# A 21st weight slot in the MoE ring, tiles that share buffers, and the last output in halves

## The chip, the cores and the metric

The kernel runs on one core of a Trainium2 chip. The metric is the device time of the whole program in microseconds (us). The kernel before takes 1551.59 us, the median of three runs (1550.2 to 1551.77). The engines are PE (matrix multiply; PEld is its weight load), DVE and ACT (elementwise work, ACT with lookup functions), POOL, and SP, which here only issues DMA transfers. An engine executes its own instructions strictly in order and waits on semaphores for the others.

## The reference

One sequence of 256 tokens with 1024 features goes through two transformer blocks, all in fp32.

```
first_block:   x += [pool_mixer(u), attention(q, k, v)] @ w_out     # u, q, k, v = rms_norm(x) @ w_in; q, k normed, rotated
               x += cross_attention(rms_norm(x), rms_norm(mem))     # 4 heads, 256 memory rows
               x += conv_ffn(rms_norm(x))                           # d_ff 2816, causal conv of width 3
second_block:  x += g1 * rms_norm([MLA attention with ctx, fourier_mix] @ w_out)
               x += g2 * rms_norm(moe(modulate(x)))
moe:           logits = h @ w_router + b_router; the top 4 of 32 experts, gates = softmax of the 4
               g = min(x_e @ w_gate[e] + b_gate[e], 7); u = clip(x_e @ w_up[e] + b_up[e], -7, 7)
               y_e = (g * sigmoid(1.702 g) * (u + 1)) @ w_down[e] + b_down[e]       # 1024 x 1024 matrices
               y[token] += gate * y_e
```

## The kernel before

**The first part** (0 to about 600 us) is everything up to the router. Its weights come in chunks of 1 MB through a ring of four slots. ACT and DVE split each chunk into a high part `wh` (L325) and a low part `wl` (L326), in two half chunks each, and PE multiplies with three matmuls per product (`ah*wh`, `al*wh`, `ah*wl`; L432 to L434 and L439 to L441). The work is written as a list of steps, and a scheduler turns the list into one fixed order per engine at build time. SP's loads use eight DMA semaphores in turn, so that a load also waits for the one eight loads before it. Among the first steps are the query and key norms of the attention: DVE reduces squares (L575), takes a reciprocal square root (L306 to L314), scales a PSUM bank `ps_a` into `qn` (L581), which frees the bank, and rotates it (L595 to L600). A little later come the softmax of the second pair of heads (L622 to L640, exponentials on ACT at L636), and the pool mixer: ACT copies `pooled` out of PSUM twice (L681), and PE multiplies each copy with `poolw` (L690).

**The MoE part** (from about 600 us to the end) is a loop over 32 experts. Each has 12 chunks of 1 MB: four of w_gate, four of w_up, four of w_down. They are streamed in that order through a ring of 20 slots (`slots`, L1482), whose memory becomes free piece by piece as the first part ends: `b1`, `b2` and `b3` are opened as pools close, `a` is the ring of the first part, `x` one more slot. `load_to` (L1491, DMA at L1504) issues the next load on SP after the last matmul that reads the slot's old chunk. For each expert `hidden` (L1602) does eight short bias matmuls (L1608) and 64 matmuls of 128x512 on gathered tokens (L1615), and DVE and ACT make the SwiGLU from two PSUM tiles (`hg`, `hs`, `hu`, L1621 to L1627); `turned` transposes the result (L1634) and copies it into `aT` (L1635); `project` does 32 matmuls (L1647); ACT copies into `z` (L1720). Every second expert, `add_y` (L1656) adds two experts' results into four PSUM banks that stay open for the whole part, and `part` gathers the next pair's tokens (L1558). `extra` (L1659) runs for an expert with more than 64 tokens; it does so once here (33 groups of 64 matmuls at L1615 in all).

**The end** (L1722 to L1737): for each half of the tokens, the last `add_y`, ACT's squares `ysq` (L1729), DVE's product with the gate (L1730), the reciprocal square root, one DVE operation of 128x1024 that scales and adds the residual (L1735), and one 512 KB store (L1737).

Small tensors that are kept all the time (`con`: identity, ones, two index rows, a triangle; `vec`, `qkb`, `wrt`) lie in the pool `keep`. The working tiles of the MoE part lie in the pool `mw`, where tiles of one tag share that tag's buffers.

Of the kernel before, what the change touches and what calls it, by code (L numbers as in the profile page):

```python
# [15 lines left out]
ALU = mybir.AluOpType  # L16
# [19 lines left out]
for _n, _w in (("mix_g", 8), ("xattn_g", 8), ("mem_g", 8), ("ffn_g", 8), ("pre_g", 8), ("pool_s", 4),  # L36
# [4 lines left out]
NVEC = _o  # L41


CONS = {"con": (("ident", 128), ("ones", 128), ("iota1", 64), ("iota32", 32), ("upper", 128)),
        "conA": (("band", 4 * 384), ("mask", 256), ("rope_c", 128), ("rope_s", 128)),
        "conM": (("dft", 2 * 512), ("cc", 128), ("sc", 128), ("ax_c", 64), ("ax_s", 64))}
CON = {}
# [207 lines left out]
def network(ctx: ExitStack, tc: tile.TileContext, A):  # L255
# [28 lines left out]
        return new(pools["stage"], shape, dt, **kw)  # L284

    con = {"con": new(keep, [P, NCON["con"]], name="con")}
    vec = new(keep, [P, NVEC], name="vec")

    def C(name, n, off=0, rows=slice(None)):
        t, o = CON[name]  # L290
# [39 lines left out]


    open_pool("tail", side="right")()
    open_pool("base", side="right")()
    open_pool("psum", space=bass.MemoryType.PSUM)()

# [5 lines left out]
    W = {}  # L341

    con["conA"] = new(keep, [P, NCON["conA"]], name="conA", tag="k8a")
    qkb = new(keep, [P, 128 + NE], name="qkb")
    qkg = qkb[:, :128].rearrange("p (a b) -> p a b", a=2)
    brt = qkb[:, 128:]
    wrt = new(keep, [P, KD, NE], name="wrt")
    bexp = new(keep, [P, 512], name="bexp")
    cT = new(pools["tail"], [P, 8, 32], name="cT", bufs=1)
    wf = new(pools["tail"], [P, 2, P], name="wf", bufs=1)  # L350
# [4 lines left out]
    def late_loads():  # L355
# [5 lines left out]
    load(xT[:, :4], A["xT"][:, :4])()  # L361
    beside = {0: [load(xT[:, 4:], A["xT"][:, 4:])],
              1: [load(con["con"], A["con"]),
                  load(qkb, bass.AP(tensor=A["qkb"].tensor, offset=A["qkb"].offset, ap=[[0, P], [1, 128 + NE]]))],
              3: [load(con["conA"], A["conA"])],
              4: [lambda: load(S["poolw"], A["pool_w"])(), load(cT, A["cT"])]}
# [1112 lines left out]
    seq = [(e, m, c) for e in experts for m in range(3) for c in range(4)]  # L1479
    chunk = {}  # L1480
    state = {"n": 0}
    slots = ["b1"] * RING_B[0] + ["a"] * 2 + ["b2"] * RING_B[1] + ["a"] * (RING_A - 2) + ["b3"] * RING_B[2] + ["x"]  # L1482
    rings = {"a": ring[0], "x": ringx}

    def moe_open(name):
        n = int(name[1])
        rings[name] = ctx.enter_context(tc.tile_pool(name="ring" + name, bufs=RING_B[n - 1], side="left",
                                                     reuse_waits="tile"))
        load_to((RING_B[0] + 2, RING_B[0] + 2 + RING_B[1], len(slots))[n - 1])

    def load_to(n):  # L1491
        while state["n"] < min(n, len(seq)):
# [17 lines left out]
    close_pool("tail")()  # L1510
    x4 = S["x4"]

    mw = ctx.enter_context(tc.tile_pool(name="mw", bufs=1, side="right", reuse_waits="tile"))
    pm = ctx.enter_context(tc.tile_pool(name="pm", bufs=1, space=bass.MemoryType.PSUM, reuse_waits="tile"))

# [19 lines left out]
    def select(es, b):  # L1535

        n = len(es)
        rank = rp1
        if b:
            rank = new(small, [P, 2, NE], name="rank")  # L1540
            nc.vector.tensor_scalar(rank, rp1, float(-SLOTS * b), None, op0=ALU.add)
        sel = new(mw, [P, 2, n, SLOTS], name="sel%d" % n)
        for t in range(2):
            for i, e in enumerate(es):
                nc.vector.tensor_scalar(sel[:, t, i], C("iota1", SLOTS), rank[:, t, e:e + 1], scale4[:, t:t + 1],
                                        op0=ALU.is_equal, op1=ALU.mult)
        per = 512 // (n * SLOTS)
        xs = []

        def part(q):  # L1550

            if not xs:
                xs.append(new(mw, [P, KD, n * SLOTS], name="xs%d" % n))
            ps = pbank("t", 2)
            for i in range(per):
                j = q * per + i
                for t in range(2):
                    nc.tensor.matmul(ps[:, i * n * SLOTS:(i + 1) * n * SLOTS], x4[:, t, j * P:(j + 1) * P],  # L1558
                                     sel[:, t].rearrange("p a b -> p (a b)"), start=t == 0, stop=t == 1)
            for i in range(per):  # L1560
                j = q * per + i
                src = ps[:, i * n * SLOTS:(i + 1) * n * SLOTS]
                if j % 2:
                    nc.vector.tensor_scalar(xs[0][:, j], src, A2[:, j:j + 1], sh2[:, j:j + 1], op0=ALU.mult, op1=ALU.add)
                else:
                    nc.scalar.activation(xs[0][:, j], src, AF.Identity, bias=sh2[:, j:j + 1], scale=A2[:, j:j + 1])  # L1566
            return xs[0]
        return rank, part
# [7 lines left out]
    def spread(rank, es, orders=2):  # L1576

        n = len(es)
        gps = []
        for o in range(orders):  # L1580
            gp = new(mw, [P, 2, 2, SLOTS], name="gp", bufs=2)
            for t in range(2):
                for h in range(2):
                    e = es[(h + o) % n]
                    nc.vector.tensor_scalar(gp[:, t, h], C("iota1", SLOTS), rank[:, t, e:e + 1], G[:, t, e:e + 1],
                                            op0=ALU.is_equal, op1=ALU.mult)
            gps.append(gp)

        def turn():
            ps = pbank("t", 2)  # L1590
            for o, gp in enumerate(gps):
                for t in range(2):
                    nc.tensor.transpose(ps[:, o * T + t * P:o * T + (t + 1) * P], gp[:, t].rearrange("p a b -> p (a b)"), ident)

            def kept(tag):
                gt = new(mw, [P, orders, T], name="gt", tag=tag, bufs=3 if tag == "h" else 1)
                nc.vector.tensor_copy(gt, ps[:, :orders * T].rearrange("p (o n) -> p o n", o=orders))
                return gt
            return kept
        return turn  # L1600

    def hidden(e, xs, i, used=None):  # L1602

        res = [pbank("g", 2) for _ in range(2)]
        for m, ps in enumerate(res):
            for h in range(2):
                k, r = slice(64 * m, 64 * m + 64), 64 * m + 2 * e + h
                nc.tensor.matmul(ps[64 * h:64 * h + 64, :], ident[k, r:r + 1].to_broadcast([64, SLOTS]), bexp[k, :],  # L1608
                                 start=True, stop=False)
        for m, ps in enumerate(res):  # L1610
            for c in range(4):
                w = chunk[e, m, c]
                for jj in range(2):
                    for h in range(2):
                        last = nc.tensor.matmul(ps[64 * h:64 * h + 64, :], xs[:, 2 * c + jj, i * SLOTS:(i + 1) * SLOTS],  # L1615
                                                w[:, jj, 512 * h:512 * h + 512], start=False, stop=c == 3 and jj == 1)
                if used is not None:
                    load_to(used + 4 * m + c + 1 + len(slots))
            if m == 0:
                g = new(mw, [P, 512], name="hg", tag="h", bufs=3)  # L1620
                nc.vector.tensor_scalar(g, ps, 7.0, None, op0=ALU.min)  # L1621
                s = new(mw, [P, 512], name="hs", tag="h", bufs=3)
                nc.scalar.activation(s, g, AF.Sigmoid, scale=1.702)  # L1623
                nc.vector.tensor_tensor(g, g, s, op=ALU.mult)
        u = new(mw, [P, 512], name="hu", tag="h", bufs=3)
        nc.vector.tensor_scalar(u, res[1], 7.0, -7.0, op0=ALU.min, op1=ALU.max)  # L1626
        nc.vector.scalar_tensor_tensor(g, u, 1.0, g, op0=ALU.add, op1=ALU.mult)  # L1627
        return g, last.ins
# [30 lines left out]
    def extra(e, b, inner=None):  # L1659

        rank, xs = select_all([e], b)
        a, last = hidden(e, xs, 0)
        if inner:
            with tc.issue_after(last):
                tc.mark_branch_hint_location(inner, "LikelyTaken", [PE])
        z = new(mw, [P, 512], name="zx", tag="h", bufs=3)
        nc.scalar.activation(z, project(e, turned(a)), AF.Copy)
        gt = spread(rank, [e], 1)()("h")
        for t in range(2):
            for h in range(2):  # L1670
                r = slice(64 * h, 64 * h + 64)
                nc.tensor.matmul(yb[t][h], gt[r, 0, t * P:(t + 1) * P], z[r, :], start=False, stop=False,
                                 skip_group_check=True)
# [50 lines left out]
    for t in range(2):  # L1724
        s = new(small, [P, 2], name="cs_s")
        add_y(gt, z, t, True)
        for h, ps in enumerate(yb[t]):
            c = slice(512 * h, 512 * h + 512)
            nc.scalar.activation(new(mw, [P, 512], name="ysq", tag="h", bufs=3), ps, AF.Square, accum_out=s[:, h:h + 1])  # L1729
            nc.vector.tensor_tensor(y[:, t, c], ps, S["gate", 1][:, c], op=ALU.mult)  # L1730
        s2 = new(small, [P, 1], name="lat_s")
        nc.vector.tensor_tensor(s2, s[:, 0:1], s[:, 1:2], op=ALU.add)  # L1732
        r2 = rms_scale(s2, D, 1, "y")
        y3 = y[:, t].rearrange("p (q j) -> p q j", j=KD)
        nc.vector.scalar_tensor_tensor(y3, y3, r2, x4[:, t].rearrange("p (j q) -> p q j", j=KD),  # L1735
                                       op0=ALU.mult, op1=ALU.add)
        nc.sync.dma_start(out[t * P:(t + 1) * P, :], y[:, t])  # L1737


def arrays_of(i):  # L1740
# [48 lines left out]
```

## Time and profile before

| what | value |
|---|---|
| median of three runs | 1551.59 us |
| the profiled execution's own time, and its span | 1554.47 us, 1552.5 us |
| mean granted PE clock over the span | 0.983 |
| PE busy | 1465.9 us, 94% |
| DVE, ACT busy | 603.9 us, 39%; 431.3 us, 28% |
| DMA | 514.82 MB, mean 332 GB/s |

All durations below come from the profiled execution, which took 1554.47 us: 1552.5 us of span and 1.97 us around it. In the profile's 40 slices PE is at 8 or 9 tenths from the first to the last, the DMA engines are at 9 tenths only from the 17th slice on (the MoE weights, about 425 GB/s), and DVE and ACT, at 5 to 8 tenths in the first third, drop to 1 or 2 in the MoE part. A wait row names who released the waiting engine; only waits on the engine that the others follow cost time.

### The profile page before, as it was taken

The page shows a single profiled execution, that of the slowest core. Times are in us where ns is not written, and L with a number is a line of the kernel's source. Part 1 is how long each engine was busy: PE and PEld are TensorE (multiplying, and loading weights), DVE is VectorE, ACT ScalarE, POOL GpSimd, SP SyncE. Part 2 cuts the span into 40 slices and gives each one's busy share as a digit, 9 for nine tenths or more (in the row PEclk, how much of TensorE's full clock was granted, in tenths as well). Part 3 has the DMA queues.
Part 4 walks back from the last instruction along what each step waited for, and adds up shares of the span by engine and source line. Part 5 has one row for each costly group of instructions (what it writes and reads, how often), then busy time and mean ns, then how long its engine had stood idle before and what let it go on. Part 6 is the DMA issues. An engine that isn't in the chain of part 4 may idle for free. (4 is left out here: it accounts for less than half of the span.)

```text
span 1552.5 us, 20127 instructions
## 1 busy us (share of the span) xinstructions
PE 1465.9 (94%) x7985; PEld 831.0 (54%) x7985; DVE 603.9 (39%) x1436; ACT 431.3 (28%) x781; POOL 5.1 (0%) x13
## 2 busy tenths in 40 slices
PE   7999999999999998999999999999899999999996
PEld 5787888789998765333433333333334333333332
DVE  7859668666767465122212112112121122121113
ACT  5545655544547542111101111101111011011111
POOL 0000000000000000000000000000000000000000
PEclk9989999999999998999999999999999999999999
DMA  9645465886532448999999999999999999999993
GB/s 345 234 159 173 153 222 194 316 300 230 190 123 94 163 170 334 388 425 425 426 424 427 424 426 426 424 425 426 408 415 425 425 426 424 426 425 426 424 426 148
DMA packets 72883, 514.82 MB, mean 332 GB/s; under 512 B 8112, under 2 KB 8880, under 8 KB 11920
## 3 DMA queue, kind: packets, MB, share of 16 engines
q1 hardware_dynamic: 71712, 507.80, 80.8%
q0 software_dynamic: 1008, 4.78, 0.8%
q8 instruction: 110, 1.80, 0.4%
q14 instruction: 53, 0.43, 0.1%
HBM read 511.50 MB, written 1.05 MB: 330 GB/s over the span
## 5 line engine op out<-in xcount | busy, mean ns | idle before, releaser
L1615 PE MATMUL p_g<-w,xs 128*64 128x512 f32 x2112 | 461.1, 594 | 0.7 <-issue 0.7
L1615 PEld LDWEIGHTS p_g<-w,xs 128*64 128x64 f32 x2112 | 148.7, 137 | 310.8 <-issue 295.8
L1647 PE MATMUL p_t<-w,aT 128*64 128x512 f32 x1056 | 235.4, 598 | 2.2 <-ACT aT L1635 2.2
L326 DVE TENSOR_TENSOR wl<-w,wh 128x1024 fp32r<-128x1024 f32 (+3 forms) x150 | 173.1, 1178 | 50.2 <-ACT wh L325 50.0
L325 ACT ACTIVATE wh<-w 128x1024 fp32r<-128x1024 f32 (+3 forms) x150 | 146.8, 1016 | 132.9 <-issue 39.0
L1621 DVE TENSOR_SCALAR hg<-p_g 128x512 f32<-128x512 f32 x33 | 22.8, 692 | 378.9 <-PE p_g L1615 378.9
L1647 PEld LDWEIGHTS p_t<-w,aT 128*64 128x64 f32 x1056 | 73.2, 137 | 149.3 <-issue 130.1
L439 PE MATMUL ps_a<-wh,ah 128*128 128x512 f32 (+3 forms) x240 | 92.1, 387 | 12.7 <-ACT wh L325 11.1
L432 PE MATMUL ps_m<-ah,wh 128*128 128x256 f32 x352 | 101.6, 289 | 1.4 <-ACT wh L325 1.4
L1623 ACT ACTIVATE hs<-hg 128x512 f32<-128x512 f32 x33 | 20.8, 629 | 289.9 <-DVE hg L1621 289.9
L434 PE MATMUL ps_m<-ah,wl 128*128 128x256 f32 x352 | 100.4, 285 | 0.0
L433 PE MATMUL ps_m<-al,wh 128*128 128x256 f32 x352 | 100.4, 285 | 0.0
L1720 ACT ACTIVATE z<-p_t 64x512 f32<-64x512 f32 x63 | 37.3, 592 | 207.5 <-PE p_t L1647 207.1
L441 PE MATMUL ps_a<-wl,ah 128*128 128x512 f32 (+3 forms) x240 | 92.3, 385 | 0.0
L440 PE MATMUL ps_a<-wh,al 128*128 128x512 f32 (+3 forms) x240 | 91.8, 383 | 0.0
L1626 DVE TENSOR_SCALAR hu<-p_g 128x512 f32<-128x512 f32 x33 | 22.8, 692 | 154.7 <-PE p_g L1615 154.7
L1656 PE MATMUL p_y<-z,gt 128*128 128x512 f32 x128 | 63.9, 605 | 18.8 <-ACTq L1680 18.1
L1558 PE MATMUL p_t<-sel,x 128*128 128x128 f32 (+1 forms) x544 | 70.7, 285 | 11.2 <-ACT aT L1635 11.2
L1558 PEld LDWEIGHTS p_t<-sel,x 128*128 128x128 f32 x544 | 64.7, 195 | 28.6 <-issue 14.6
L1566 ACT ACTIVATE xs<-p_t,modT,A 128x128 f32<-128x128 f32 (+1 forms) x68 | 30.8, 453 | 158.9 <-PE p_t L1558 146.7
L432 PEld LDWEIGHTS ps_m<-ah,wh 128*128 128x128 f32 x352 | 68.1, 194 | 9.3 <-issue 3.4
L434 PEld LDWEIGHTS ps_m<-ah,wl 128*128 128x128 f32 x352 | 68.1, 194 | 2.4 <-DVE wl L326 0.8
(368 smaller groups left out, 1787.1 us busy)
## 6 DMA issues: line engine op xcount, KB each, us to landing
w<-w_gate_dram SPq DMA_DIRECT2D x128, 1024.0 KB, 19.6
w<-w_up_dram SPq DMA_DIRECT2D x128, 1024.0 KB, 19.5
w<-w_down_dram SPq DMA_DIRECT2D x127, 1024.0 KB, 19.6
w<-wall_dram SPq DMA_DIRECT2D x89, 1024.0 KB, 4.9
w<-wall_dram SPq DMA_DIRECT2D x4, 768.0 KB, 4.1
w<-wall_dram SPq DMA_DIRECT2D x3, 576.0 KB, 3.8
w<-wall_dram SPq DMA_DIRECT2D x2, 640.0 KB, 3.9
xT<-xT_dram SPq DMA_DIRECT2D x2, 512.0 KB, 7.7
```

Of the source, the lines that this page charges most:

```text
L325: nc.scalar.activation(hi, src, AF.Copy)
L326: nc.vector.tensor_tensor(lo, src, hi.bitcast(F32), op=ALU.subtract)
L432: nc.tensor.matmul(o, sh, mh, start=start, stop=False, **kw)
L433: nc.tensor.matmul(o, sh, ml, start=False, stop=False, **kw)
L434: nc.tensor.matmul(o, sl, mh, start=False, stop=stop, **kw)
L439: nc.tensor.matmul(o, a, wh, start=start, stop=False)
L440: nc.tensor.matmul(o, b, wh, start=False, stop=False)
L441: return nc.tensor.matmul(o, a, wl, start=False, stop=stop)
L1558: nc.tensor.matmul(ps[:, i * n * SLOTS:(i + 1) * n * SLOTS], x4[:, t, j * P:(j + 1) * P], sel[:, t].rearrange("p a b -> p (a b)"), start=t ...
L1615: last = nc.tensor.matmul(ps[64 * h:64 * h + 64, :], xs[:, 2 * c + jj, i * SLOTS:(i + 1) * SLOTS], w[:, jj, 512 * h:512 * h + 512], start= ...
L1647: nc.tensor.matmul(po[64 * h:64 * h + 64, :], s, w[:, jj, o:o + 512], start=c == 0 and jj == 0, stop=c == 3 and jj == 1)
L1656: nc.tensor.matmul(yb[t][h], gt[:, h, t * P:(t + 1) * P], z[:, h], start=False, stop=stop, skip_group_check=True)
```

## The change

- `con` is cut in two: `con` keeps the identity and the 64-wide index row, a new tensor `conR` holds the ones, the 32-wide index row and the triangle. `conR` gets a load of its own at the start, right behind `con`'s.
- `conR`, `vec`, `qkb` and `wrt` move from `keep` to `tail`, a pool that is closed before the MoE part.
- In the MoE part tiles are put under shared tags: `sel1` with `gp`, `xs1` with `aT`, `hu` and `zx` with `hs`, the `gt` of an extra pass with `hg`, `ysq` with `xs2`. Before, `hg`, `hs`, `hu`, `zx` and `ysq` went round three buffers of the tag `h`.
- The memory won becomes a 21st ring slot, `c`, opened when `tail` is closed; its first load is issued then.
- The last operation on DVE is done in two halves of 128x512 for each half of the tokens, and each half is stored by itself (four stores of 256 KB, not two of 512 KB).

```diff
-CONS = {"con": (("ident", 128), ("ones", 128), ("iota1", 64), ("iota32", 32), ("upper", 128)),
+CONS = {"con": (("ident", 128), ("iota1", 64)),
+        "conR": (("ones", 128), ("iota32", 32), ("upper", 128)),
...
-    vec = new(keep, [P, NVEC], name="vec")
...
     open_pool("tail", side="right")()
+    vec = new(pools["tail"], [P, NVEC], name="vec", bufs=1)
+    con["conR"] = new(pools["tail"], [P, NCON["conR"]], name="conR", bufs=1)
...
-    qkb = new(keep, [P, 128 + NE], name="qkb")
+    qkb = new(pools["tail"], [P, 128 + NE], name="qkb", bufs=1)
...
-    wrt = new(keep, [P, KD, NE], name="wrt")
+    wrt = new(pools["tail"], [P, KD, NE], name="wrt", bufs=1)
...
               1: [load(con["con"], A["con"]),
+                  load(con["conR"], A["conR"]),
...
-    slots = [... + ["b3"] * RING_B[2] + ["x"]
+    slots = [... + ["b3"] * RING_B[2] + ["x", "c"]
...
-        load_to((RING_B[0] + 2, RING_B[0] + 2 + RING_B[1], len(slots))[n - 1])
+        load_to((RING_B[0] + 2, RING_B[0] + 2 + RING_B[1], len(slots) - 1)[n - 1])
...
     close_pool("tail")()
     x4 = S["x4"]
+    rings["c"] = ctx.enter_context(tc.tile_pool(name="ringC", bufs=1, side="left", reuse_waits="tile"))
+    load_to(len(slots))
...
-                g = new(mw, [P, 512], name="hg", tag="h", bufs=3)
+                g = new(mw, [P, 512], name="hg")
...
-                s = new(mw, [P, 512], name="hs", tag="h", bufs=3)
+                s = new(mw, [P, 512], name="hs")
...
-        u = new(mw, [P, 512], name="hu", tag="h", bufs=3)
+        u = new(mw, [P, 512], name="hu", tag="hs")
...
-            nc.scalar.activation(new(mw, [P, 512], name="ysq", tag="h", bufs=3), ps, AF.Square, accum_out=s[:, h:h + 1])
+            nc.scalar.activation(new(mw, [P, 512], name="ysq", tag="xs2"), ps, AF.Square, accum_out=s[:, h:h + 1])
...
-        nc.vector.scalar_tensor_tensor(y3, y3, r2, x4[:, t].rearrange("p (j q) -> p q j", j=KD),
-                                       op0=ALU.mult, op1=ALU.add)
-        nc.sync.dma_start(out[t * P:(t + 1) * P, :], y[:, t])
+        for h in range(2):
+            q = slice(64 * h, 64 * h + 64)
+            nc.vector.scalar_tensor_tensor(y3[:, q], y3[:, q], r2, x4[:, t].rearrange("p (j q) -> p q j", j=KD)[:, q],
+                                           op0=ALU.mult, op1=ALU.add)
+            nc.sync.dma_start(out[t * P:(t + 1) * P, 512 * h:512 * h + 512], y[:, t, 512 * h:512 * h + 512])
```

Line numbers grow by 2 or 3 in the first part and by 3 to 7 in the MoE part (L581 becomes L584, L681 becomes L684, L1504 becomes L1507, L1737 becomes L1744). The scheduler places the same steps differently in the first 95 us; from there to the end PE's instructions come in the same order in both kernels. Three places follow.

The first place is DVE at about 33 to 40 us, the query norm beside the split of a weight chunk; `wl` is the low part of half a chunk, `rs_y` the reciprocal square root, `hs` a sum of squares. Before:

```order
L326 TENSOR_TENSOR wl<-w,wh 128x1024 [waits DMAHW3_49,PE_49,Activation_49]
L314 SCALAR_TENSOR_TENSOR rs_y_269<-rs_t_271,rs_y_269 128x8 [waits DVE_49]
L313 TENSOR_TENSOR rs_t_301<-rs_t_301,rs_h_300 128x8 [waits DVE_49]
L326 TENSOR_TENSOR wl<-w,wh 128x1024 [waits Activation_49]
L580 TENSOR_SCALAR rs_y_269<-rs_y_269,R_x_195 128x8 [waits DVE_49]
L314 SCALAR_TENSOR_TENSOR rs_y_299<-rs_t_301,rs_y_299 128x8 [waits DVE_49]
L575 TENSOR_REDUCE hs_402<-hsq 128x8 [waits Activation_49]
L581 TENSOR_TENSOR qn<-ps_a,rs_y_269 128x512 [waits DVE_49]
L580 TENSOR_SCALAR rs_y_299<-rs_y_299,R_x_195 128x8 [waits DVE_49]
```

And now:

```order
L326 TENSOR_TENSOR wl<-w,wh 128x1024 [waits DMAHW4_49,PE_49,Activation_49]
L583 TENSOR_SCALAR rs_y_271<-rs_y_271,R_x_197 128x8 [waits DVE_49]
L583 TENSOR_SCALAR rs_y_301<-rs_y_301,R_x_197 128x8 [waits DVE_49]
L584 TENSOR_TENSOR qn<-ps_a,rs_y_271 128x512 [waits DVE_49]
L326 TENSOR_TENSOR wl<-w,wh 128x1024 [waits Activation_49]
L598 TENSOR_TENSOR rot<-qn,rope 128x512 [waits DVE_49]
L600 TENSOR_TENSOR rotb<-qn,rope 128x8x32 x2
L578 TENSOR_REDUCE hs_404<-hsq 128x8 [waits Activation_49]
L603 TENSOR_TENSOR rot<-rot,rotb 128x512 [waits DVE_49]
```

The scaling `qn`, which empties a PSUM bank, stood behind both `wl` and behind the reduction at L575; now it stands behind the first `wl` alone, with the second `wl` and the reduction behind it.

The second place is ACT at about 73 to 82 us, the softmax of the second heads (`s`, scaled by `sm_b` from DVE) beside the pool mixer (`pooled`). Before:

```order
L652 ACTIVATE pt_689<-ps_m 128x4x128 [waits PE_49]
L681 ACTIVATE pooled<-ps_m 128x512 [waits PE_49]
L636 ACTIVATE s_653,sm_s_660<-s_653,sm_b_658 128x256 [waits DVE_49,Activation_49]
L636 ACTIVATE s_653,sm_s_660<-s_653,sm_b_658 128x256 x3
L325 ACTIVATE ah<-ps_a 128x512 [waits PE_49]
L636 ACTIVATE s_674,sm_s_681<-s_674,sm_b_679 128x128 [waits DVE_49,Activation_49]
L636 ACTIVATE s_674,sm_s_681<-s_674,sm_b_679 128x128 x3
L681 ACTIVATE pooled<-ps_m 128x512 [waits PE_49]
L328 ACTIVATE ah<-ps_m,vec 128x256 [waits PE_49] x4
```

And now:

```order
L639 ACTIVATE s_655,sm_s_662<-s_655,sm_b_660 128x256 [waits DVE_49,Activation_49]
L639 ACTIVATE s_655,sm_s_662<-s_655,sm_b_660 128x256 x3
L325 ACTIVATE ah<-ps_a 128x512 [waits PE_49]
L684 ACTIVATE pooled<-ps_m 128x512 [waits PE_49] x2
L639 ACTIVATE s_676,sm_s_683<-s_676,sm_b_681 128x128 [waits DVE_49,Activation_49]
L639 ACTIVATE s_676,sm_s_683<-s_676,sm_b_681 128x128 x3
L328 ACTIVATE ah<-ps_m,vec 128x256 [waits PE_49] x4
```

The first `pooled` went down behind four exponentials, the second went up ahead of the four narrow ones, so that the two stand together; the four `ah` of the pool mixer now stand behind the narrow exponentials too. On DVE at the same place one `wl`, which stood ahead of the reduction that gives `sm_b`, now stands behind it.

The third place is SP at the start of the MoE part, where the ring is filled for the first time; the DMAHW semaphores are those of the loads eight places before. Before:

```order
L1504 DMA w<-w_up_dram 128x2048 [waits DMAHW1_49]
L1504 DMA w<-w_up_dram 128x2048 [waits DVE_49,DMAHW2_49,PE_49,Activation_49]
L1504 DMA w<-w_down_dram 128x2048 [waits DMAHW3_49,PE_49]
L1504 DMA w<-w_down_dram 128x2048 [waits DMAHW4_49,PE_49]
L1504 DMA w<-w_down_dram 128x2048 [waits DMAHW5_49,PE_49]
```

And now:

```order
L1507 DMA w<-w_up_dram 128x2048 [waits DMAHW2_49]
L1507 DMA w<-w_up_dram 128x2048 [waits DVE_49,DMAHW3_49,PE_49,Activation_49]
L1507 DMA w<-w_down_dram 128x2048 [waits DMAHW4_49,DVE_49]
L1507 DMA w<-w_down_dram 128x2048 [waits DMAHW5_49,PE_49]
L1507 DMA w<-w_down_dram 128x2048 [waits DMAHW6_49,PE_49]
```

The last load of the first fill, the one of slot `x` (it waits for DVE, PE and ACT), is followed by one more that waits for DVE and no matmul, the load of slot `c`; only the loads behind it wait for PE to free a slot.

## Rows read from the trace of the kernel before

**Rows 1.** The page's first line:

```profile
span 1552.5 us, 20127 instructions
```

**Rows 2.** Waits of PE, 640 to 1540 us (releaser: total us, times, longest):

```profile
PE p_y L1656 <- ACTq L1680: 18.1, 14, 1.3
```

**Rows 3.** Waits of PE's weight load, 640 to 1540 us:

```profile
PEld p_g L1615 <- DMA w<-w_down_dram: 6.3, 13, 0.8
```

**Rows 4.** Stretches (length, busy us per engine, granted clock, DMA share, GB/s):

```profile
1000.00:1100.00 100.00, 96.35 (x472) 36.97 (x470) 18.87 (x49) 11.75 (x22) 0.00 (x0) 1.00 1.01 425
...
1520.00:1530.00 10.00, 7.64 (x38) 2.77 (x36) 2.58 (x4) 1.23 (x2) 0.00 (x0) 1.00 0.49 206
```

**Rows 5.** Tile w, 1060 to 1092 us: matmuls of one expert, landing of loads:

```profile
L1615 PE MATMUL p_g<-w,xs x64: 592/592/643, 1062.8 to 1076.2; 128*64 128x512 f32 x64
...
DMA to landing us min/median/max: 19.6/19.6/20.0
```

**Rows 6.** Timeline of SP, the loads of the same expert (start, length, count):

```profile
1046.66 5.20 SPq L1504 DMA_DIRECT2D w<-w_up_dram  x3
```

**Rows 7.** Waits of SP, 640 to 1540 us:

```profile
SPq L1504 <- DMA w<-w_up_dram: 179.9, 87, 3.0
...
SPq L1504 <- PE p_g L1615: 133.4, 95, 11.9
```

**Rows 8.** Timeline of SP at the start of the MoE part:

```profile
615.45 5.48 SPq L1504 DMA_DIRECT2D w<-w_down_dram  x4
```

**Rows 9.** Timeline, 34 to 38 us (start, length, [idle before <-releaser]):

```profile
34.24 1.22 DVE L326 TENSOR_TENSOR wl<-w,wh 128x1024 fp32r<-128x1024 f32 x1
...
35.59 0.68 DVE L575 TENSOR_REDUCE hs<-hsq 128x8 f32<-128x512 f32 x1
...
36.19 0.69 DVE L581 TENSOR_TENSOR qn<-ps_a,rs_y 128x512 f32<-128x512 f32 x1
...
37.02 0.47 PE L439 MATMUL ps_a<-wh,ah 128*128 128x512 f32 x1 [0.96 <-ACT wh L325]
```

**Rows 10.** Timeline, 72 to 82 us:

```profile
72.46 1.22 DVE L326 TENSOR_TENSOR wl<-w,wh 128x1024 fp32r<-128x1024 f32 x1
...
75.31 0.51 ACT L636 ACTIVATE s<-s,sm_b 128x256 f32<-128x256 f32 x1 [0.57 <-DVE sm_b L633]
...
79.31 0.58 ACT L681 ACTIVATE pooled<-ps_m 128x512 f32<-128x512 f32 x1
...
79.94 0.70 PE L690 MATMUL ps_m<-pooled,poolw 128*128 128x256 f32 x2 [2.44 <-ACT pooled L681]
...
80.82 0.72 PE L690 MATMUL ps_m<-pooled,poolw 128*128 128x256 f32 x2 [0.18 <-DVE al L329]
```

**Rows 11.** Stretches around that place:

```profile
78.00:80.00 2.00, 0.06 (x1) 0.07 (x1) 1.97 (x4) 2.00 (x10) 0.00 (x0) 1.00 0.93 373
...
82.00:91.00 9.00, 8.08 (x37) 5.79 (x38) 1.66 (x3) 2.92 (x6) 0.53 (x1) 0.50 0.06 24
```

**Rows 12.** Timeline of PE in the last expert:

```profile
1528.24 0.72 PE L1634 MATMUL p_t<-con,hg 128*128 128x128 f32 x4 [1.61 <-DVE hg L1627]
```

**Rows 13.** Timeline of SP in the first 10 us:

```profile
5.45 1.39 SPq L379 DMA_DIRECT2D w<-wall_dram  x2
9.02 0.33 SPq L353 DMA_DIRECT2D conA<-conA_dram  x1
```

**Rows 14.** Timeline, the last operations:

```profile
1546.34 2.67 SPq L1737 DMA_DIRECT2D out_dram<-y  x2
...
1546.68 1.97 DVE L1735 SCALAR_TENSOR_TENSOR y<-y,rs_y,x 128x1024 f32<-128x1024 f32 x1
```

**Rows 15.** Timeline of DVE, the nearest operation of half width:

```profile
588.66 1.42 DVE L1359 SCALAR_TENSOR_TENSOR x<-xT,rs_y,x 128x512 f32<-128x512 f32 x2
```

**Rows 16.** DMA issues, first 40 us and last 7 (size, us to landing):

```profile
vec<-vec_dram SPq DMA_DIRECT2D x1, 118.5 KB, 2.1
...
out_dram<-y SPq DMA_DIRECT2D x2, 512.0 KB, 2.6
```

More of the change, by code (lines that the diff above doesn't have):

```diff
@@ L1481, in network @@
     state = {"n": 0}
-    slots = ["b1"] * RING_B[0] + ["a"] * 2 + ["b2"] * RING_B[1] + ["a"] * (RING_A - 2) + ["b3"] * RING_B[2] + ["x"]
+    slots = ["b1"] * RING_B[0] + ["a"] * 2 + ["b2"] * RING_B[1] + ["a"] * (RING_A - 2) + ["b3"] * RING_B[2] + ["x", "c"]
     rings = {"a": ring[0], "x": ringx}
@@ L1541, in select @@
             nc.vector.tensor_scalar(rank, rp1, float(-SLOTS * b), None, op0=ALU.add)
-        sel = new(mw, [P, 2, n, SLOTS], name="sel%d" % n)
+        sel = new(mw, [P, 2, n, SLOTS], name="sel%d" % n, tag=None if n == 2 else "gp", bufs=None if n == 2 else 2)
         for t in range(2):
@@ L1552, in part @@
             if not xs:
-                xs.append(new(mw, [P, KD, n * SLOTS], name="xs%d" % n))
+                xs.append(new(mw, [P, KD, n * SLOTS], name="xs%d" % n, tag=None if n == 2 else "aT"))
             ps = pbank("t", 2)
@@ L1595, in kept @@
             def kept(tag):
-                gt = new(mw, [P, orders, T], name="gt", tag=tag, bufs=3 if tag == "h" else 1)
+                gt = new(mw, [P, orders, T], name="gt", tag=tag, bufs=1)
                 nc.vector.tensor_copy(gt, ps[:, :orders * T].rearrange("p (o n) -> p o n", o=orders))
@@ L1665, in extra @@
                 tc.mark_branch_hint_location(inner, "LikelyTaken", [PE])
-        z = new(mw, [P, 512], name="zx", tag="h", bufs=3)
+        z = new(mw, [P, 512], name="zx", tag="hs")
         nc.scalar.activation(z, project(e, turned(a)), AF.Copy)
-        gt = spread(rank, [e], 1)()("h")
+        gt = spread(rank, [e], 1)()("hg")
         for t in range(2):
```

## The prediction

> **What bounds the kernel now.** I read the slices and the engine table first, then the waits of PE for the MoE part, then what stands behind each wait in the timeline. The span is 1552.5 us [rows 1] and the profiled execution took 1554.47 us, 2.88 above the median of 1551.59; the sum below is made against 1554.47 and its difference carried over to the median.
>
> Three fifths of the span is the MoE part. There two resources look full: PE is busy 96.35 us of 100 and the DMA engines show a share of 1.01 at 425 GB/s [rows 4]. The reader must decide which of the two the other follows. The waits of PE decide it: its longest entry is 18.1 us in 14 pieces, and that releaser is ACT's sequencer at an expert's branch, not a transfer [rows 2]; no entry of PE names a DMA. Only the weight load names one, 6.3 us in 13 pieces of at most 0.8 us [rows 3], and the weight load runs beside the matmuls, which show no gap for it. So the weights arrive in time, and a full DMA queue is loads running ahead, not loads that PE lacks.
>
> How far ahead, at the tightest place I found: the last w_up load of one expert is issued at 1046.66 + 5.20 - 0.33 = 1051.5 us (0.33 being the length of one issue) [rows 6] and lands 19.6 us later [rows 5], at 1071.1. The 64 matmuls of the expert begin at 1062.8 and take 13.4 us [rows 5]; the eighth chunk of eight is reached at 1062.8 + 13.4 x 7/8 = 1074.5. The lead is about 3.4 us: thin, but there. Both kinds of SP wait occur, for an older load (179.9 us for w_up alone) and for PE to free a slot (133.4 us) [rows 7], so the ring is full in some stretches and DMA-paced in others.
>
> **The change part by part.**
>
> The 21st slot. It adds one chunk of lead: 1.05 MB at 425 GB/s [rows 4] is 2.5 us. Its first load goes out before the first release by PE, for which SP waited until 615.45 us [rows 8]; it now waits for DVE's last reader of the closed pool instead, on the same queue, and what stands behind it is only the loads that wait for PE anyway. A lead that grows from 3.4 to 5.9 us where nothing waits is worth 0. The bounds: up to -5.0 (2.5 us twice, at the two places where the lead is thin, in the middle and in the last expert), if PE did wait where the rows show none; up to +0.3 if the DVE release came later than PE's. I take 0.
>
> Shared buffers. `hu` now waits for `hs` to be read and `hg` for the transposes of the expert before; in PE's order both are long past (32 matmuls of `project` lie between). The four squares at the end now share one buffer, so each waits for the one before it on the same engine, which ended anyway. I take +0.1, between 0 and +0.3.
>
> The last output. DVE's operation of 128x1024 takes 1.97 us [rows 14] and ends the chain; two halves cost the same elements and one more start each. Nearest from the other side: an operation of 128x512 elsewhere, two of which take 1.42 us together [rows 15], and that would make it shorter by 0.55 us in each half of the tokens, -1.1; but its operands are not read with a stride, as these are. I take +0.1 per added operation, +0.2 (between -1.1 and +0.3). The last store shrinks from 512 to 256 KB. A store of 512 KB lands after 2.6 us, a lone load of 118.5 KB after 2.1 [rows 16]; on the line between them 256 KB takes 2.3, so -0.3. The first half is stored one half operation earlier and is gone by then. I take -0.4, between 0 and -0.6.
>
> One rule of the Trainium skill speaks against this edit: its page "DMA: Bandwidth & Descriptors" (section Bandwidth, under Measured) wants transfers of at least 1 MiB, since each has a fixed cost, about 2.0 us by its section "Anatomy of one DMA". The trace has 2.6 us for 512 KB where that section's formula has 3.2, so the formula is high here. By it the smaller last store would still save 0.6 us, since the fixed cost of the others lies beside DVE's work; the sum would be -1.2 in place of -1.0.
>
> The new order in the first 95 us. First place: PE stood 0.96 us, until 37.02, ahead of the first matmul of a new chunk [rows 9]. The row names ACT's `wh`, but that operation was under way a microsecond before; what ended just ahead is `qn`, at 36.19 + 0.69 = 36.88, which frees the PSUM bank. In the new order `qn` stands ahead of the second `wl` (1.22 us) and of the reduction (0.68 us), so it ends some 1.8 us sooner and the stall of 0.96 can go altogether. What is late next is the rotation and the second `wl`, since DVE has no idle time there, and PE meets them later in the same stretch. I take less than half of the stall, -0.4 (between -1.1 and +0.3).
>
> Second place: PE stood 2.44 us until 79.94 for the second `pooled`, at 79.31 on ACT [rows 10]. In the new order `sm_b` no longer stands behind a `wl` of 1.22 us, less a small mask operation that moves ahead of it, so the wide exponentials start about 0.7 us sooner than 75.31, and the two `pooled` follow at about 77.1, the second 1.6 us sooner. But the third matmul pair waits for `al`, hence for an `ah` that now stands behind the narrow exponentials (78.2 to 79.7), and so comes at 80.7 against 80.82 [rows 10]. Only the fourth gains more. I take -0.5 (between -2.4 and +0.6).
>
> The added load of `conR`. The number of bytes is unchanged and one issue of 0.4 us is added among loads that are queued: 0, between -0.4 and +0.4.
>
> The sum: 0 + 0.1 + 0.2 - 0.4 - 0.4 - 0.5 + 0 = -1.0 us, 1553.5 for an execution like the profiled one, 1550.6 for the median. PE is the bound from the first part to the last expert, so what the front gains passes through, as nothing in the MoE part waits for a clock time.
>
> **The rivals.**
>
> The clock stays up (faster). Around the second place PE does 0.06 us of work in 2 us, and in the 9 us after 82 it runs at a granted clock of 0.50, the lower level [rows 11]. Those 8.08 busy us would take half at the full level, 4.0 us, of which I count 3.5 because some of it waits for ACT. A gap of 1.61 us late in the kernel [rows 12] lies in a stretch at 1.00 [rows 4], and the longest gap left by my working is 80.7 - 78.9 = 1.8 us. For it: the gap is cut in two. Against: between 77 and 82 PE does as little work as before. Time: 1550.6 - 3.5 = 1547.1. Chance 0.20.
>
> The ring does matter (faster). The weight load's pieces [rows 3] are then the tips of waits that the modelled ends of the matmuls hide, and 2.5 us come back at each thin place: 1545.6 to 1548.1. Against: the matmuls of such an expert keep one duration, 592 ns at the median and 643 at most [rows 5]. Chance 0.06.
>
> The start slips (slower). One more load ahead turns the semaphores by one: the second of the two chunk loads that went out from 5.45 us on, at about 6.5, has to wait for what `conA`'s load waited for, until 9.02, and `conA`'s own load goes out some 2.5 us later than 9.02 as well [rows 13]. If the split of that chunk and the rotation tables then come late one after the other on DVE, that is up to 5.0 us, 1555.6. It decides when a landing passes the moment DVE reaches the tile. Against: the DMA engines have work throughout, so a later issue only changes whose bytes come first. Chance 0.06.
>
> The change does only what its end shows (the front's gains are given back on DVE): +0.1 + 0.2 - 0.4 = -0.1, 1551.5. It counts as no change, and is the other part of the forecast's side.
>
> **How the numbers follow.** A measurement of this kernel can tell 0.2%, 3.1 us, from no change. The forecast and the last rival hold 0.68 together and both lie inside it: same 0.68. The clock and the ring give faster 0.20 + 0.06 = 0.26, the slipping start slower 0.06. The forecast's own range is 1549.0 to 1552.6. For 8 in 10 it has to take in most of the clock's case: 1546.6 to 1552.8.
>
> **What would show it.** Right: no PE wait on a DMA in either kernel; SP's first load behind the first fill goes out before PE's first release, and PE's MoE part has the same length; the gap at 37 us gone or halved; the last store landing about 2.3 us after its issue. Wrong: a granted clock of 1.00 from 82 to 91 us, a MoE part shorter by 2 us or more, or DVE standing for a transfer between 20 and 40 us.

## The result: slower by half a per cent, because the DMA itself became slower

The changed kernel takes 1558.94 us, the median of seven runs (1554.17 to 1564.53), against 1550.2 for the kernel before in seven runs (1548.28 to 1551.77). The ratio is 1.0053, with a 95% interval of 1.0039 to 1.0067: 8.2 us slower by the ratio (the two medians lie 8.7 us apart). The forecast was 1550.6, in a range of 1546.6 to 1552.8, with a chance of 0.06 for slower.

The profiled execution of the changed kernel took 1554.88 us, 0.4 us more than the one of before. This near tie hides two large terms with opposite signs, so the stretches have to be read, not the span.

The DMA first. The page's first line and the row of the DMA rate in 40 slices, of the changed kernel:

```profile
span 1553.1 us, 20145 instructions
...
GB/s 332 248 167 182 136 256 188 322 305 218 180 107 120 136 216 378 398 419 419 419 419 420 418 421 418 420 419 420 417 420 419 419 419 419 418 414 420 412 419 163
```

And three stretches of it (length, busy us of PE, PEld, DVE, ACT and POOL, granted clock, DMA share, GB/s):

```profile
1000.00:1100.00 100.00, 97.35 (x474) 37.09 (x472) 18.39 (x43) 11.22 (x21) 0.00 (x0) 1.00 1.01 419
1510.00:1520.00 10.00, 8.34 (x36) 1.94 (x32) 1.38 (x2) 0.63 (x1) 0.00 (x0) 1.00 1.00 412
1520.00:1530.00 10.00, 6.56 (x30) 2.01 (x28) 1.38 (x2) 0.16 (x1) 0.00 (x0) 1.00 0.63 259
```

The DMA engines are as full as before, at a share of 1.01, but they move 419 GB/s where they moved 425 [rows 4]. A load lands after 19.8 us in the median where it took 19.6 [rows 5]. In the trace's packet records a piece of 8 KB takes 309 ns in nearly all cases before (700 to 1500 us, 41,222 pieces) and 312 ns in the median after (40,694 pieces, mean 315.3, about one in five 319). The bytes, their number and the eight loads in flight are the same. At these rates a chunk of 1.05 MB takes 2.50 us instead of 2.47, 0.035 us more, and there are 384 of them.

What this does to PE. Waits of PE from 640 to 1545 us in the changed kernel, releaser, total us, times and longest (waits on ACT, DVE and a sequencer left out, but for the largest):

```profile
PE p_y L1661 <- ACTq L1685: 18.1, 14, 1.3
...
PE p_g L1620 <- DMA w<-w_up_dram: 3.7, 8, 0.7
...
PE p_g L1620 <- DMA w<-w_gate_dram: 1.1, 2, 0.6
```

The first line is that of before to the tenth [rows 2]; the two below it are new. They understate the loss, since a matmul that starts late is drawn long or merely later. The weight load shows it better; the waits of PEld in the same stretch:

```profile
PEld p_g L1620 <- DMA w<-w_up_dram: 18.0, 23, 1.6
PEld p_g L1620 <- DMA w<-w_down_dram: 7.6, 21, 0.8
PEld p_g L1620 <- DMA w<-w_gate_dram: 6.2, 10, 1.4
```

Before, the line for w_down was 6.3 us with 0.8 at most [rows 3]; the two others in this stretch were these:

```profile
PEld p_g L1615 <- DMA w<-w_gate_dram: 4.0, 14, 0.3
...
PEld p_g L1615 <- DMA w<-w_up_dram: 2.2, 4, 0.8
```

They were pieces beside running matmuls. Now w_up stands at 18.0 us, in pieces of up to 1.6. The last expert of the changed kernel, the matmuls of PE (start, length, count, idle time and its releaser):

```profile
1508.80 3.77 PE L1620 MATMUL p_g<-w,xs 128*64 128x512 f32 x16
1513.12 1.94 PE L1620 MATMUL p_g<-w,xs 128*64 128x512 f32 x8 [0.56 <-DMA w<-w_gate_dram]
1515.61 1.94 PE L1620 MATMUL p_g<-w,xs 128*64 128x512 f32 x8 [0.55 <-DMA w<-w_gate_dram]
1518.10 1.94 PE L1620 MATMUL p_g<-w,xs 128*64 128x512 f32 x8 [0.55 <-DMA w<-w_up_dram]
1520.59 1.94 PE L1620 MATMUL p_g<-w,xs 128*64 128x512 f32 x8 [0.56 <-DMA w<-w_up_dram]
1523.05 1.94 PE L1620 MATMUL p_g<-w,xs 128*64 128x512 f32 x8 [0.53 <-DMA w<-w_up_dram]
1525.54 1.94 PE L1620 MATMUL p_g<-w,xs 128*64 128x512 f32 x8 [0.55 <-DMA w<-w_up_dram]
```

Eight matmuls, one chunk, then a wait: PE goes at the pace of the loads, one chunk in 2.49 us. The 64 matmuls take from 1508.80 to 1527.48, 18.7 us. In the kernel before, those of the last expert took 13.95 us:

```profile
1512.68 13.95 PE L1615 MATMUL p_g<-w,xs 128*64 128x512 f32 x64
```

The traces also give the lead of every chunk, from the landing of its load to the start of the first matmul that reads it. Before, the smallest is 3.9 us, for the load issued at 1051.5 us. In the changed kernel it is 0.04 us, which is no lead at all, for several chunks between 1039 and 1099 us and again in the last three experts.

The other term is at the start. The MoE part's first weight matmul comes at 606.9 us in this execution and came at 613.5 in the profiled one of before, 6.6 us sooner. Less than 1 us of it is the new order: the run with the halves alone (below), which has the old order and stays at the lower clock as briefly around 82 us, starts its 450th PE instruction at 99.06 us, and the changed kernel at 98.77. The rest goes with the granted clock. Before, it was at its lower level, 0.50, for 10.2 us from 81.4 us on, and for 10.2 us again between 460 and 474 us; in the changed kernel's execution it was there for 3.4 us at each of these places. The stretch from 82 to 91 us, which had 0.50 before [rows 11]:

```profile
82.00:91.00 9.00, 7.93 (x59) 6.83 (x59) 1.66 (x3) 2.87 (x5) 0.53 (x1) 0.84 0.29 95
```

From the first weight matmul to the first square on ACT at the end it is 933.4 us in the changed kernel (606.9 to 1540.3) and 926.0 before (613.5 to 1539.5). So the changed kernel lost 7.4 us in the MoE part: 2.7 by the start of the last expert's weight matmuls, and 4.7 in these.

The two places of the new order, as the changed kernel runs them. DVE at 33 to 37 us:

```profile
33.50 1.22 DVE L326 TENSOR_TENSOR wl<-w,wh 128x1024 fp32r<-128x1024 f32 x1
...
34.91 0.68 DVE L584 TENSOR_TENSOR qn<-ps_a,rs_y 128x512 f32<-128x512 f32 x1
35.51 1.22 DVE L326 TENSOR_TENSOR wl<-w,wh 128x1024 fp32r<-128x1024 f32 x1
```

`qn` ends at 35.59 where it ended at 36.88 [rows 9], and PE's matmul at 36.11 shows no idle time: the 0.96 us are gone. Then the second place, ACT and PE:

```profile
74.32 0.51 ACT L639 ACTIVATE s<-s,sm_b 128x256 f32<-128x256 f32 x1 [1.01 <-DVE sm_b L636]
...
76.79 1.06 ACT L684 ACTIVATE pooled<-ps_m 128x512 f32<-128x512 f32 x2
```

```profile
77.42 1.18 PE L693 MATMUL ps_m<-pooled,poolw 128*128 128x256 f32 x4 [0.50 <-ACT pooled L684]
80.77 1.40 PE L693 MATMUL ps_m<-pooled,poolw 128*128 128x256 f32 x4 [2.18 <-DVE al L329]
```

The gap of 2.44 us [rows 10] is cut into 0.50 and 2.18, and the third pair starts at 80.77, against 80.82 before and 80.7 in the prediction. And the end, DVE and SP, and the landing of the four stores:

```profile
1545.39 2.08 DVE L1742 SCALAR_TENSOR_TENSOR y<-y,rs_y,x 128x512 f32<-128x512 f32 x2
1546.50 3.78 SPq L1744 DMA_DIRECT2D out_dram<-y  x4
...
1547.83 2.09 DVE L1742 SCALAR_TENSOR_TENSOR y<-y,rs_y,x 128x512 f32<-128x512 f32 x2
```

```profile
out_dram<-y SPq DMA_DIRECT2D x4, 256.0 KB, 2.0
```

Two halves take 2.09 us where one operation took 1.97 [rows 14], and a store of 256 KB lands after 2.0 us where one of 512 KB took 2.6 [rows 16]. The four squares on ACT come ahead of that. Before and now, from the chain of work that ended last:

```profile
1539.51 0.70 ACT ysq L1729 x2
```

```profile
1540.29 0.70 ACT ysq L1734 x2
1541.01 0.15 ACT ysq L1734
```

From the first square to the end of the span it is 12.8 us after (1540.29 to 1553.1) and 13.0 before (1539.51 to 1552.5): 0.2 us shorter. The squares themselves, which now share one buffer, start 0.72 us apart where they started 0.57 to 0.62 apart; from the first to the fourth that is 0.38 us more.

### The profile page after: what moved, and what is told of

It reads as the page before. It is cut to its first block, busy times and chain, and to the rows that moved or that the text cites. A ratio compares the mean times of both kernels' runs of the same rounds, so it can differ in the third digit from the quotient of the medians.

```text
span 1553.1 us, 20145 instructions
## 1 busy us (share of the span) xinstructions
PE 1463.8 (94%) x7985; PEld 824.6 (53%) x7985; DVE 603.8 (39%) x1438; ACT 431.8 (28%) x781; POOL 5.1 (0%) x13
## 3 DMA queue, kind: packets, MB, share of 16 engines
HBM read 511.50 MB, written 1.05 MB: 330 GB/s over the span
## 6 DMA issues: line engine op xcount, KB each, us to landing
w<-w_gate_dram SPq DMA_DIRECT2D x128, 1024.0 KB, 19.8
w<-w_up_dram SPq DMA_DIRECT2D x128, 1024.0 KB, 19.8
w<-w_down_dram SPq DMA_DIRECT2D x127, 1024.0 KB, 19.8
```

## The experiments

Slow DMA pieces with unchanged bytes pointed at where they are written. By the build's own addresses all 20 slots of before start at a multiple of 256 bytes in a partition; the change takes 3776 bytes out of `keep`, which lies ahead of the ring, and all 21 slots then start 64 bytes past one (57600 becomes 53824). That is theory A. Theory B was that 21 slots, or the loads' new order, make the queue slow by themselves; theory C, that this was chance of one execution. The pads below move, besides the slots, the small tiles that lie behind `con`; the large working tiles of the MoE part (`aT`, `hg`, `hs`, `hu`) keep their addresses.

**The changed kernel again, unedited.**

> The changed kernel once more, unedited. In its first trace a weight packet of 8 KB takes 312 to 319 ns where it took 309 before, the DMA moves 419 GB/s in the MoE part where it moved 425, and PE waits for weights (4.8 us named, 8 us lost against the start of the MoE part). Theory A (the slots' SBUF addresses: 256-byte multiples before, 64 past one now): 419 GB/s again, 1554 to 1562 us, ratio 1.003 to 1.007. Theory B (21 slots or the loads' new order): the same. Theory C (chance of one execution, a neighbour on the memory): 425 GB/s, ratio about 1.000.

1557.23 us (six runs), ratio 1.0046 (1.0031 to 1.0061); 419 to 420 GB/s, pieces of 312 ns in the median. C is out.

**A pad of 192 bytes.**

```diff
-    con = {"con": new(keep, [P, NCON["con"]], name="con")}
+    con = {"con": new(keep, [P, NCON["con"] + 48], name="con")[:, :NCON["con"]]}
```

> The changed kernel with 192 bytes more ahead of the ring, so that all 21 slots start at multiples of 256 bytes again; nothing else moves. Theory A: 425 GB/s in 700 to 1500 us, packets of 309 ns, no PE wait on a weight transfer above 1 us, 1546 to 1550 us, ratio 0.997 to 1.000. Theory B: 419 GB/s and 1554 to 1562 us, as without the pad. Theory C: as the changed kernel, whatever that does in these rounds.

1549.31 us (12 runs), ratio 0.9986 (0.9973 to 1.0000). One stretch of its trace:

```profile
1000.00:1100.00 100.00, 97.71 (x480) 37.56 (x480) 18.63 (x45) 11.19 (x21) 0.00 (x0) 1.00 1.01 426
```

426 GB/s, pieces of 309 ns, no wait of PE on a transfer from 640 us on, and the last expert's 64 matmuls in one row:

```profile
1506.70 13.95 PE L1620 MATMUL p_g<-w,xs 128*64 128x512 f32 x64
```

One number in one line takes away the whole loss; 21 slots, shared buffers and halves all stay. A holds, B falls.

**The changed kernel without the 21st slot** (`["x", "c"]` becomes `["x"]`, the pool `ringC` goes).

> The changed kernel without the 21st slot (its memory stays unused; addresses, shared buffers, halves and the order of the start as in the change). Theory A: still 419 GB/s, and a lead smaller by one chunk: 1556 to 1564 us, 1 to 3 us slower than the changed kernel. Theory B: 425 GB/s and 1548 to 1551 us.

1561.56 us (six runs), ratio 1.0073 (1.0053 to 1.0093), 419 GB/s. The slot was no cause. The median is 4.3 us above that of the changed kernel on the same chip, but the mean clock was 0.0022 lower too, which by the 1.1 us for each 0.001 of these six runs is 2.4 us; and the profiled MoE parts, up to the last expert's weight matmuls, are only 0.4 and 1.2 us longer than in the two traces of the changed kernel. Where weights are late the slot seems to help by some 1 or 2 us; these runs do not settle it.

**The kernel before, 64 bytes off.**

```diff
-    con = {"con": new(keep, [P, NCON["con"]], name="con")}
+    con = {"con": new(keep, [P, NCON["con"] + 16], name="con")[:, :NCON["con"]]}
```

> The kernel before with 64 bytes more ahead of the ring, so that its 20 slots start 64 bytes past a multiple of 256; nothing else is changed. Theory A: 419 GB/s, PE waits for weights, 1554 to 1560 us, ratio 1.002 to 1.006. Theories B and C: 425 GB/s, 1550 us, ratio 1.000.

1560.16 us (six runs), ratio 1.0064 (1.0050 to 1.0079). Its trace:

```profile
1000.00:1100.00 100.00, 96.30 (x470) 36.47 (x470) 18.50 (x44) 11.20 (x21) 0.00 (x0) 1.00 1.01 420
```

Without any part of the change, 64 bytes make the kernel before as slow as the changed one, and 2.9 us more. It lacks the 21st slot and the shorter end; how much of the 2.9 us is due to either was not separated.

**64 bytes of pad in the changed kernel** (`+ 16`): 128 past a multiple of 256.

> The changed kernel with 64 bytes more ahead of the ring: slots start 128 bytes past a multiple of 256. If 128 bytes are enough: 425 GB/s, packets of 309 ns, about 1549 us. If it takes 256: 419 GB/s, packets above 309 ns, 1554 to 1562 us. A half-way packet (310 to 311 ns) would put it at 1550 to 1555.

1557.39 us (six runs), ratio 1.0054 (1.0029 to 1.0078), pieces of 312 ns in the median, 420 GB/s. 128 bytes past a multiple are slow too. 192 bytes past one, and addresses between two multiples of 64, were not run.

**Half of the weight matmuls left out**, so that the DMA alone sets the MoE part, without and with the 192-byte pad.

```diff
-                for jj in range(2):
+                for jj in (1,):
```

> The changed kernel with half of the weight matmuls left out (every second row group of each chunk), so that PE takes some 30 us for a pair of experts and the MoE part is set by the DMA alone. Slots 64 bytes past a multiple of 256. Theory A: 419 GB/s from 600 us to the end; 377 chunks of 1.05 MB after the first fill take 377 x 2.50 = 943 us. If reading by PE were needed for the slow packets: fewer of them, and nearer to 425 GB/s.

> The same with the 192-byte pad, slots at multiples of 256. Theory A: 425 GB/s, and 377 x (2.50 - 2.465) = 11 to 14 us less than without the pad, all of it DMA. If the address mattered only beside a busy PE: the same time as without the pad.

The medians are 1554.9 us (four runs) and 1543.88 (five runs), 11.0 us apart; the two profiled spans, 1551.7 and 1538.0, 13.7. Their stretches, each from its own trace:

```profile
1000.00:1100.00 100.00, 72.53 (x280) 24.30 (x278) 17.10 (x42) 10.56 (x20) 0.00 (x0) 0.84 1.01 420
```

```profile
1000.00:1100.00 100.00, 73.04 (x290) 25.45 (x286) 18.38 (x43) 11.16 (x21) 0.00 (x0) 0.86 1.01 426
```

This is the price of the address by itself: 11 to 14 us, as expected; the rate falls as far with PE busy at 73 of 100 us as at 97. Of it the changed kernel shows 7.4 in its trace: 384 x 0.035 = 13.4 us, less a lead that in the padded kernel is 5.6 us at its smallest (below), is 7.8.

**The 21st slot with the pad, without and with the slot.**

> The changed kernel with the 192-byte pad and without the 21st slot: what the slot is worth once its address costs nothing. Theory A1 (aligned, PE never waits for a weight, so the slot is worth nothing): as with the pad and 21 slots, 1549 us, ratio 0.9985, no PE wait on a weight. Theory A2 (the start of the MoE part is some 6 us sooner than in the first trace of before, where the smallest lead was 3.4 us, so 20 slots are short again by 2 to 3 us): 1551 to 1553 us, with PE waits on w_up of 1 to 3 us around 1060 us.

> The changed kernel with the 192-byte pad once more, beside the next one on the same chip: 425 GB/s, no PE wait on a weight, ratio 0.997 to 1.000.

> The same without the 21st slot. Theory A1 (aligned, the smallest lead is 4 us, the slot is worth 0): within 1 us of the one with 21 slots on the same chip. Theory A2 (the slot is worth the 2.7 us that lay between the two on different chips): slower than it by 2 to 3 us at the same mean clock.

With 20 slots 1551.89 us, ratio 1.0013 (1.0002 to 1.0024), on another chip than the first run with the pad; then on one chip, 12 runs each, 1550.34 with 21 slots, 0.9996 (0.9982 to 1.0010), and 1550.88 with 20, 1.0006 (0.9993 to 1.0019). In the traces no PE wait on a weight shows up with 20 slots either. The two lie 0.5 us apart on the same chip, within what the runs can tell: A1, the slot is worth nothing that these runs can tell once nothing waits. It does lengthen the lead: the smallest one is 5.6 and 5.9 us in the two padded traces with 21 slots, 3.9 and 3.7 with 20. The 2.6 us that I saw between two chips were mostly not the slot's: with 20 slots the mean clock was 0.0028 below that of the kernel before on the same chip, with 21 slots 0.0003.

**`conR` alone.** `con` is cut in two and loaded in two, both kept where `con` was, so the ring does not move and the engines' order of the first 95 us is the changed kernel's.

> The kernel before with con cut in two and conR loaded by itself, both kept where con was: the engines' order of the first 95 us is that of the changed kernel, the ring's addresses are those of before. The prediction put this order at -0.9 us (between -3.5 and +0.9): ratio 0.9994. A rival: what the first trace gained at the start (MoE part 6.6 us sooner) was the granted clock of that one execution and not the order: ratio 0.9990 to 1.0010 and, over the executions, the same mean clock as before. The other rival: the order itself changes how often the clock falls, mean clock off by 0.001 or more, 1 us for each 0.001.

1551.79 us (12 runs), ratio 1.0002 (0.9989 to 1.0015). The gain of 0.9 us that I had put here does not show. Mean clocks: 0.9852 here against 0.9867 for the kernel before on the same chip. In the five sets with the new order and aligned slots the mean clock is 0.0003 to 0.0028 lower than that of before beside it, and in each set the time rises by 1.0 to 1.2 us for each 0.001 that the clock falls. So the new order may cost as much through the clock as it saves in stalls. The direction is the same five times, but three of the five are compared with the same runs of before, and the size is not settled. A straight line through the runs of each set, read at one clock (0.987), puts the padded kernel with 21 slots at 1547.9 and 1548.1 us and the kernel before at 1550.3; whether these 2 us are a gain or lie in where the clock falls was not tried.

**The halves alone**, on the kernel before.

> The kernel before with the last output in halves and nothing else. By the changed kernel's trace (the last operations 0.12 us longer for each half of the tokens, 0.67 us less from the last of them to the end of the span) it gains 0.3 to 0.6 us: ratio 0.9996 to 0.9998, below what the rounds can tell; the trace has to show it.

1549.68 us (12 runs), ratio 0.9994 (0.9978 to 1.0009); the trace repeats 2.09 us for two halves and 2.0 us to landing. From the first square to the end its trace has 12.55 us, where the kernel before has 13.0 and the changed kernel 12.8. So the halves gain 0.5 us, and in the changed kernel the shared buffer of the squares takes about half of it back. The sign cannot be told from the runs, only from the traces.

## Why the prediction was wrong, point by point

- **The step that failed** is in the first term, the 21st slot with the tiles that leave `keep`: "1.05 MB at 425 GB/s". I carried the DMA rate of before over as a constant. The move has no instruction, so the comparison of orders shows nothing of it, and I gave it no term; but it shifts every slot by 3776 bytes, to 64 past a multiple of 256, and 425 GB/s became 419. The runs with pads show this cause by itself, in both directions.
- **The numbers to price it were all there.** The smallest lead was 3.4 us by my working and 3.9 by the trace (I had counted the 64 matmuls from first start to last start, and the eighth chunk begins a little later); with the new slot I expected 5.9, and the padded kernel has 5.6 and 5.9. A chunk that takes 0.035 us more costs 192 x 0.035 = 6.7 us over the 16 experts ahead of the tightest place, and the second half loses as much again. Less the 5.6 us of lead that is 7.8 us, where the trace lost 7.4. I had written that the lead is "thin, but there" and then asked only what happens if it grows, not what could eat it: 1.4% of the DMA rate does.
- **That PE waits for no DMA means no price for faster loads; it says nothing on slower ones.** PE and the DMA engines stood at 96 and 101 of 100 [rows 4]. A lead of 3.9 us over 192 chunks is 0.02 us a chunk, 0.8% of its 2.47 us: the side that does not bind was one per cent from binding. The weight load's row, too, was read too narrowly: the prediction says that it names one DMA, 6.3 us, and the view has four more such lines, 16.3 us in all, though no piece is longer than 0.8.
- **Why such addresses are slow** no run shows. The Trainium skill has the rule that comes nearest: "DMA: Bandwidth & Descriptors", section "How a descriptor splits into AXI transactions", where a piece that does not start at a multiple of 256 bytes needs a first transaction from the boundary below it; the Trainium skill says this of what a transaction reads, and here it is the address written to that counts. An estimate by it: 8192 bytes at 64 past a multiple are 33 transactions instead of 32 and 258 beats instead of 256, 0.8 to 3.1% more. The runs lie between: 1.0% for the median piece (312 against 309 ns), 1.6% for the mean (315.3 against 310.4) and 1.4% for the rate. Two things in the traces go beyond it. Counted in beats, slots at 128 past a multiple (260) should be slower still, but their pieces take no longer (mean 314.8 ns). And the same misaligned slots took 309 ns for loads up to about 597 us and, after the queue ran empty, again from 634 to 648 us. So the extra work shows only in some stretches of a full queue; what switches it was not tried.
- **The 21st slot worth 0** was right for an aligned ring (0.5 us between 20 and 21 slots, not told from none).
- **Shared buffers** at +0.1: no new wait of PE shows in the MoE part but those on weights. But the squares at the end, which I let pass because each follows the one before it "on the same engine, which ended anyway", start 0.10 to 0.15 us later each: +0.38 us from the first to the fourth, above the range of 0 to +0.3. All ten traces with the shared buffers have it, and none of the four without.
- **The last output** at -0.2: the added operations cost +0.12 each as taken (+0.1), the store saved 0.6, not 0.4. The 0.6 is what the prediction named by the formula of the Trainium skill ("DMA: Bandwidth & Descriptors", section "Anatomy of one DMA"); that formula is for DMAs issued by GpSimd, and for these stores, issued by SP, it is 0.6 us too high (2.6 for 256 KB, where the trace has 2.0). The end as a whole is 0.2 us shorter in the profiled pair, and 0.5 with the halves alone.
- **The front** at -0.9: the two places went nearly as worked out (the stall at 37 us gone, 80.77 against 80.7), but the sum did not come through: alone it measures +0.3 us, between -1.7 and +2.3. In the profiled executions the 0.96 us are given back soon, as PE's 200th instruction starts at 57.48 us after and at 57.38 before; at 99 us some 0.3 us is gained (99.06 against 98.77, above). The rival "the clock stays up" took one execution for the rule. After the gap near 80 us two of the runs with the old order (the halves alone, and the kernel before 64 bytes off) were at the lower clock for 3.4 us, and one with the new order (64 bytes of pad) for 10.2; so the higher clock of the profiled execution, 0.84 from 82 to 91 us, was no gain of the change. The time of the kernel before goes between 1546 and 1558 us with its mean clock.
- **The rival for slower**, the slipping start, did not cost anything: `conA`'s load went out at 11.89 us, 2.9 later than before, but DVE's only wait between 20 and 40 us is 0.6 us for PE, the same as before, and none is for a transfer.

With the pad, the change does what the forecast said: 0.9986 (0.9973 to 1.0000) and 0.9996 (0.9982 to 1.0010), faster than the changed kernel by 8 us and not to be told from the kernel before. That the sum of -1.0 us lies inside these intervals says little for it: by the traces its terms come to about -0.5 (front -0.3, end -0.2, slot 0), and the runs cannot tell the two apart.

## What to carry to other kernels

Where a stream of loads is within a few per cent of being the bound, the start addresses of its buffers are a term of their own: read them from the build before and after every change of a tile ahead of them, and keep them at multiples of 256 bytes, which was enough here. A resource at a share of 1.0 that nobody waits for has a lead; price a change in units of that lead, from both sides. And where the clock of one execution moves the time by several microseconds, no difference between two profiled executions is a gain of the change until it has repeated.

## What the runs showed of the hardware that I had not expected

- Writing 8 KB pieces to addresses 64 or 128 bytes past a multiple of 256 lowered a full DMA stream from 425 or 426 to 419 or 420 GB/s, in all six traces with such slots and in none of the eight with aligned ones.
- In the slow stretches with slots 64 bytes past a multiple, pieces that follow each other on one DMA engine mostly repeat 319, 312, 312, 312 ns, counted with the 4-byte piece that ends an engine's share of a load. (The engine of a piece is inferred: it is the one whose last piece ends where this one starts.) At 128 bytes past, the durations vary from 309 to 324 ns, and long ones again come four pieces apart. At about 648 us of the changed kernel's trace the slow pieces go from few to nearly all within about 2 us.
- The time follows the mean granted clock closely: 35 runs of the kernel before on one chip go from 1546.07 to 1558.06 us, and 1.2 us go with 0.001 of clock (correlation -0.94). So two profiled executions whose mean clocks differ by 0.005, as those of the kernel before and the changed kernel do (0.983 and 0.988), cannot be compared by their spans.
